# A two-block transformer forward pass on one core: tokens scaled and split without GpSimd, six units ahead, attention scores of two heads issued alternately, norm spreads placed later, and the last K tiles done by token tile

## The chip, the cores and the metric

The kernel runs on 1 core of one Trainium2 chip. The metric is the device time of one execution in microseconds (us), the median of several runs. TensorE does matmuls, VectorE (DVE), ScalarE (ACT) and GpSimd (POOL) the elementwise work; SyncE (SP) and, after the change, ScalarE too, issue DMA transfers between HBM and the on-chip memory (SBUF). Matmuls write to PSUM, eight banks of 128 x 512 fp32.

## The reference, cut to what matters

256 tokens of width 2048 go through two blocks. The first has a mixer (an 8-head gated linear scan and a 16-head chunked attention, merged by two sigmoid gates) and a feed-forward layer `square(relu(u @ w_up)) @ w_down` of width 8192. The second has a spatial-gating branch, a 16-head neighbourhood attention, two gates again, and a feed-forward layer of width 5504 with a 3-tap convolution and a SiLU gate. Each block begins with an RMS norm of the tokens, and each feed-forward layer too; a last norm ends the block:

```python
def rms_norm(x, w):
    xf = x.astype(jnp.float32)
    y = xf * lax.rsqrt(jnp.mean(xf * xf, axis=-1, keepdims=True) + EPS)
    return (y * w.astype(jnp.float32)).astype(x.dtype)
...
h = h + mixer_block(rms_norm(h, norm_mix_w[l]), ...)
u = rms_norm(h, norm_mlp_w[l])
h = h + jnp.square(jax.nn.relu(u @ w_up[l])) @ w_down[l]
```

Everything is fp32. An attention score is `q . k / 8 + bias`, one product of 64 features per head.

## The kernel before, in words

**Precision.** A product of two fp32 matrices is made of three fp32r products. Each weight tile `raw` that a DMA brings is split into a high part `wh` (ACT, line 104) and the rest `wl` (DVE, line 105); activations are split the same way, and `mm3` (lines 122 to 131) or `group` (lines 161 to 184) multiply high by high, high by low and low by high.

**Order of the work.** `Builder.prog` is a list of `Half`s and of functions. A `Half` is one weight tile of 128 x 1024 (512 KB) and the matmuls on it: half of a *unit* (128 output features for all 256 tokens, eight K tiles, `unit_b`) or two K tiles of a *group* (512 output features for two token tiles, `group`). `run` (lines 264 to 306) walks the list; one Half is one *tick*. In a tick it issues the DMA of the Half six ticks ahead (four `raw` buffers), steps the background generators (the scan, the attentions), splits the weights of the Half three ticks ahead (four `wh`/`wl` buffers), emits the Half's matmuls, and then `flush`es what became due: evictions out of PSUM, each `delay` ticks after its unit ended, and generators that were begun earlier. All engines run through their own instructions in this order and wait for each other by semaphores.

**PSUM.** Pool `mm` has four banks for units and groups, pool `sm` four for all small products (scores, transposes, norm spreads).

**The start.** `begin` (lines 400 to 482) loads the tokens, feature-major, in pieces of two and four K tiles. `split` (lines 419 to 428) scales each K tile by the norm weight: GpSimd writes the scaled tokens `xg` (line 423), ACT or DVE write their high part `xs` (lines 427, 425), and DVE subtracts (line 428). GpSimd also adds the squares for the norm (lines 457, 474). The norm factor itself is applied later, at eviction. The first eight units (`hf`) run with `wave=4`: the first halves of four units, then their second halves.

**Norm spreads.** The per-token factor is made in columns (`rsqrt_cols`) and must be spread over a row for feature-major evictions: `cols_to_row` (lines 386 to 397) makes `diag` (DVE, line 392), multiplies it by ones (TensorE, line 393, `row`) and copies the result to `R`. It is called by `new_r` (before each feed-forward layer) and by `chain` in `second`, each three ticks after the layer began and in steps of one tick; in `chain` two scalings of the whole `h` (line 990) stand ahead of it.

**Attention.** `attention` (lines 711 to 778) makes one head per step, a step every 1.4 ticks. The scores of head `i` are two matmuls of 64 features (line 737), on partitions 0 to 63 for even heads and 64 to 127 for odd ones, into one `sm` bank. Then follow the transposes of head `i-2` (line 744), and in even steps the outputs of two heads (line 751), issued alternately into the two halves of the output partitions.

**The end.** The second feed-forward layer goes in chunks of `FF2_CHUNKS` hidden tiles: `up(c+1)` stands ahead of `down(c)`. `down` of the last chunk evicts with `finish` (squares, multiplication by the norm weight), and `last` makes the norm, scales and stores.

## Time and profile before

| what | value |
| --- | --- |
| median of 3 runs | 2847.3 us (2846.12 to 2847.81) |
| the profiled execution | 2845.72 us |
| its span, first to last instruction | 2843.6 us |
| mean granted TensorE clock | 0.995 |
| busy share: TensorE, DVE, ACT, GpSimd | 98 %, 63 %, 49 %, 5 % |
| DMA | 529.52 MB, mean 186 GB/s |

The span is the time from the first to the last instruction of the core; the execution's own time is 2.1 us longer. "PE" is TensorE's matmuls, "PEld" its weight loads, which overlap them. A row of the timeline gives the start, the length, the engine, the line, the operation, its output and inputs, the count of like instructions merged, and in brackets the idle time before it with what ended that. Lengths of matmuls are from issue to the last result, so two neighbours overlap; their distance from start to start is what they cost.

### The profile page before, as it was taken

Reading aid. Unit: us, or ns where it says so; the run is one execution under the profiler, and the core shown is the slowest. Engines: PE = TensorE matmul, PEld = TensorE weight load, DVE = VectorE, ACT = ScalarE, POOL = GpSimd, SP = SyncE. Lnnn points to the kernel's source line nnn. Section 1 sums busy time; section 2 is a strip of 40 time slices with the busy share of each in tenths; the row PEclk is TensorE's granted clock in tenths of the full one; section 3 lists DMA queues with packets and bytes.
Section 4 is the critical chain, followed back from the end, with each engine's and each line's share of the span. In section 5 each row is a group of like instructions: output and inputs, shape, how many; then the busy total and the mean of one; then the engine's idle time right before and its main releaser. Section 6 shows DMA issues by size and latency. Waiting matters only on the chain.

```text
span 2843.6 us, 37303 instructions
## 1 busy us (share of the span) xinstructions
PE 2800.7 (98%) x14148; PEld 2352.9 (83%) x14148; DVE 1795.4 (63%) x2440; ACT 1390.7 (49%) x1922; POOL 129.2 (5%) x91
## 2 busy tenths in 40 slices
PE   7999999999999999999999999999999999999998
PEld 6889877888888888888887887788888888888886
DVE  6767565555576666666665755555558767676765
ACT  4554545444544444444464445544456545454544
POOL 5021000000000000000020000000000000000001
PEclk9999999999999999999999999999999999999999
DMA  6544565666556666666556665566656565556664
GB/s 199 189 156 142 165 192 160 187 192 219 181 183 190 191 192 187 192 190 189 192 192 200 205 195 187 155 192 192 216 174 188 186 192 186 191 187 188 190 188 160
DMA packets 147924, 529.52 MB, mean 186 GB/s; under 512 B 16544, under 2 KB 18848, under 8 KB 147232
## 3 DMA queue, kind: packets, MB, share of 16 engines
q1 hardware_dynamic: 147744, 527.14, 58.9%
q8 instruction: 111, 1.82, 0.3%
q14 instruction: 69, 0.57, 0.1%
HBM read 522.88 MB, written 4.19 MB: 185 GB/s over the span
## 4 chain that ended last, share of the span: by engine, by line
PE 97%; ACT 1%; DVE 0%; issue 0%; DMA 0%; POOL 0%; SPq 0%; ACTq 0%; DVEq 0%; POOLq 0%
PE mm L130 26%; PE mma L177 17%; PE mma L179 17%; PE mma L178 17%; PE mm L131 13%; PE mm L128 2%; PE s L737 1%; PE sc L638 1%; PE mm L127 1%; PE pt L744 1%; PE tr L196 1%; PE po L751 1%; DMA raw<-in_w_in_hf 0%; ACT wh L104 0%; DVE wl L105 0%
## 5 line engine op out<-in xcount | busy, mean ns | idle before, releaser
L105 DVE TENSOR_TENSOR wl<-raw,wh 128x1024 fp32r<-128x1024 f32 (+1 forms) x965 | 1193.6, 1239 | 963.5 <-ACT wh L104 954.1
L104 ACT ACTIVATE wh<-raw 128x1024 fp32r<-128x1024 f32 (+1 forms) x965 | 1018.1, 1057 | 1324.4 <-PE mma L178 675.2
L130 PE MATMUL mm<-u,wh 128*128 128x512 f32 x2610 | 931.0, 399 | 0.0
L131 PE MATMUL mm<-u,wl 128*128 128x256 f32 x2610 | 733.6, 281 | 0.0
L130 PEld LDWEIGHTS mm<-u,wh 128*128 128x128 f32 x2610 | 491.1, 188 | 113.1
L131 PEld LDWEIGHTS mm<-u,wl 128*128 128x128 f32 x2610 | 493.5, 189 | 8.3
L177 PE MATMUL mma<-wh,a 128*128 128x512 f32 x856 | 333.3, 389 | 0.0
L179 PE MATMUL mma<-wl,a 128*128 128x512 f32 x856 | 333.0, 389 | 0.0
L178 PE MATMUL mma<-wh,a 128*128 128x512 f32 x856 | 333.0, 389 | 0.0
L130 PE MATMUL mm<-xs,wh 128*128 128x512 f32 x600 | 220.7, 407 | 12.1 <-DVE xs L428 12.1
L178 PEld LDWEIGHTS mma<-wh,a 128*128 128x128 f32 x856 | 160.7, 188 | 33.5
L179 PEld LDWEIGHTS mma<-wl,a 128*128 128x128 f32 x856 | 160.7, 188 | 33.3
L177 PEld LDWEIGHTS mma<-wh,a 128*128 128x128 f32 x856 | 160.7, 188 | 32.8
L131 PE MATMUL mm<-xs,wl 128*128 128x256 f32 x600 | 170.4, 284 | 7.5 <-DVE wl L105 7.5
L177 PE MATMUL mma<-wh,xs 128*128 128x512 f32 x384 | 152.6, 397 | 0.0
L177 PE MATMUL mma<-wh,u 128*128 128x512 f32 x384 | 152.5, 397 | 0.0
L178 PE MATMUL mma<-wh,u 128*128 128x512 f32 x384 | 150.1, 391 | 0.0
L179 PE MATMUL mma<-wl,u 128*128 128x512 f32 x384 | 150.0, 390 | 0.0
L178 PE MATMUL mma<-wh,xs 128*128 128x512 f32 x384 | 149.7, 390 | 0.0
L179 PE MATMUL mma<-wl,xs 128*128 128x512 f32 x384 | 149.6, 390 | 0.0
L130 PEld LDWEIGHTS mm<-xs,wh 128*128 128x128 f32 x600 | 114.8, 191 | 37.9 <-DVE xs L428 13.2
L131 PEld LDWEIGHTS mm<-xs,wl 128*128 128x128 f32 x600 | 115.4, 192 | 10.5 <-DVE wl L105 8.6
(238 smaller groups left out, 3038.3 us busy)
## 6 DMA issues: line engine op xcount, KB each, us to landing
raw<-in_w_up SPq DMA_DIRECT2D x300, 512.0 KB, 3.5
raw<-in_w_down SPq DMA_DIRECT2D x212, 512.0 KB, 3.5
raw<-in_w_in_ga SPq DMA_DIRECT2D x64, 512.0 KB, 3.5
raw<-in_w_in_gb SPq DMA_DIRECT2D x64, 512.0 KB, 3.5
raw<-in_w_br SPq DMA_DIRECT2D x64, 512.0 KB, 3.5
raw<-in_w_out SPq DMA_DIRECT2D x64, 512.0 KB, 3.5
raw<-in_w_in_av SPq DMA_DIRECT2D x32, 512.0 KB, 3.6
raw<-in_w_in_hq SPq DMA_DIRECT2D x16, 512.0 KB, 3.7
```

The costliest lines, as they stand in the source:

```text
L104: nc.scalar.activation(hi, src, AF.Copy)
L105: nc.vector.tensor_tensor(lo, src, hi.bitcast(F32), ALU.subtract)
L127: nc.tensor.matmul(out[:, :T], lhsT=wl, rhs=x[:, 0, :], start=False, stop=False)
L128: nc.tensor.matmul(out, lhsT=wh, rhs=both, start=start, stop=True)
L130: nc.tensor.matmul(out, lhsT=wh, rhs=both, start=start, stop=False)
L131: nc.tensor.matmul(out[:, :T], lhsT=wl, rhs=x[:, 0, :], start=False, stop=False)
L177: nc.tensor.matmul(ps, lhsT=xt[:, 1, ts], rhs=wh[:, w], start=kt == 0, stop=False)
L178: nc.tensor.matmul(ps, lhsT=xt[:, 0, ts], rhs=wh[:, w], start=False, stop=False)
L179: nc.tensor.matmul(ps, lhsT=xt[:, 0, ts], rhs=wl[:, w], start=False, stop=kt == n_k - 1)
L196: self.nc.tensor.transpose(ps[:, j * T + tt * P : j * T + (tt + 1) * P], z[tt][:, c : c + P], self.ident)
L638: nc.tensor.matmul(ps[:, hh * P : (hh + 1) * P], lhsT=lhs, rhs=rhs, start=True, stop=True)
L737: nc.tensor.matmul(ps[:, sl[tt]], lhsT=aq[off : off + 64, j, tt * P : (tt + 1) * P], rhs=ak[off : off + 64, j, 0 : n(tt)], start=True, sto ...
```

## The change

It has five parts.

1. **Start.** ACT alone scales the tokens into `xg` (new `scaled`), DVE alone casts the high part and subtracts (`split`); GpSimd takes no part, and DVE adds the squares, later. The loads stand in another order: two weight Halves more come ahead of the last token tiles. The first wave is six units, of which two use `sm` banks, and the norm chain begins at tick 6 in place of 5.
2. **Norm spreads.** One tick later in `new_r`, two ticks later in `chain` of `second`, where the scaling of `h` now comes behind the spread, one tile per tick. The first units of a wave are evicted up to two ticks later to fit.
3. **Scores.** In even steps both heads' scores are issued, alternately, into two banks; odd steps issue none.
4. **Chunks.** `[8, 8, 8, 8, 8, 3]` becomes `[8, 8, 8, 8, 7, 2, 2]`.
5. **The last chunk** makes the four products of token tile 0 first and keeps its weights, then those of tile 1; norm, scaling and store go by token tile, and stores are issued from SP and ACT.

The diff, cut to its core:

```diff
-FF2_CHUNKS = [8, 8, 8, 8, 8, 3]
+FF2_CHUNKS = [8, 8, 8, 8, 7, 2, 2]
...
-                    box["ps"] = self.mm_p.tile([P, 512], F32, tag="mm", name=self.name("mm"))
+                    box["ps"] = self.sm("mms") if small else self.mm_p.tile([P, 512], F32, tag="mm", name=self.name("mm"))
...
+        def scaled(a, n):
+            for kt in range(a, a + n):
+                nc.scalar.activation(part(xg, kt, 1), part(x, kt, 1), AF.Copy, scale=self.cv("norm_mix_w", kt))
+
         def split(a, n):
-            tiles, j = st["x"][a // 4], a % 4
-            for kt in range(a, a + n):
-                src, g = x[kt // 8][:, kt % 8, :], self.cv("norm_mix_w", kt)
-                nc.gpsimd.tensor_scalar(xg[kt // 8][:, kt % 8, :], src, g, None, ALU.mult)
-                if kt % 2:
-                    nc.vector.tensor_scalar(tiles[:, kt % 4, 0, :], src, g, None, ALU.mult)
-                else:
-                    nc.scalar.activation(tiles[:, kt % 4, 0, :], src, AF.Copy, scale=g)
-            nc.vector.tensor_tensor(tiles[:, j : j + n, 1, :], xg[a // 8][:, a % 8 : a % 8 + n, :], tiles[:, j : j + n, 0, :].bitcast(F32), ALU.subtract)
+            hi, lo = (st["x"][a // 4][:, a % 4 : a % 4 + n, i, :] for i in range(2))
+            nc.vector.tensor_copy(hi, part(xg, a, n))
+            nc.vector.tensor_tensor(lo, part(xg, a, n), hi.bitcast(F32), ALU.subtract)
...
         load(0, 2)
+        load(2, 2)
         dma(0, 1)
-        load(2, 2)
         load(4, 4)
         dma(1)
         dma(2)
+        dma(3)
         load(8, 4)
-        dma(3)
         load(12, 4)
...
         def squares():
-            split(12, 4)
-            square(2)
-            yield
-            square(3)
-            yield
+            for q in (2, 3):
+                scaled(4 * q, 4)
+                split(4 * q, 4)
+                yield
+            for q in range(4):
+                nc.scalar.activation(part(sq, 4 * q, 4), part(x, 4 * q, 4), AF.Square)
+                if q:
+                    nc.vector.tensor_tensor(a[0], a[0], a[q], ALU.add)
+                if q % 2:
+                    yield
             for w in (512, 256):
-                nc.gpsimd.tensor_tensor(a[0][:, :w], a[0][:, :w], a[0][:, w : 2 * w], ALU.add)
+                nc.vector.tensor_tensor(a[0][:, :w], a[0][:, :w], a[0][:, w : 2 * w], ALU.add)
...
-        self.add(lambda: self.later(5, chain))
-        self.units([b("hf", "zf", h, delay=2 if h == 0 else 1) for h in range(8)], wave=4)
+        self.add(lambda: self.later(6, chain))
+        self.units([self.unit_b(w["hf"], h, x, self.ev("zf", h), max(1, 3 - h), h in (4, 5)) for h in range(8)], wave=6)
...
         for i in range(16 + 4):
+            if i < 16 and i % 2 == 0:
+                pss = [self.sm("s") for _ in range(2)]
+                for tt in range(2):
+                    for off, ps in zip((0, 64), pss):
+                        nc.tensor.matmul(ps[:, sl[tt]], lhsT=aq[off : off + 64, i // 2, tt * P : (tt + 1) * P],
+                                         rhs=ak[off : off + 64, i // 2, 0 : n(tt)], start=True, stop=True)
             if i < 16:
-                off, j = 64 * (i % 2), i // 2
-                ps = self.sm("s")
-                for tt in range(2):
-                    nc.tensor.matmul(ps[:, sl[tt]], lhsT=aq[off : off + 64, j, tt * P : (tt + 1) * P], rhs=ak[off : off + 64, j, 0 : n(tt)],
-                                     start=True, stop=True)
+                ps = pss[i % 2]
...
         self.rsqrt_cols(y, x)
         yield
+        yield
         yield from self.cols_to_row(y)
...
             self.rsqrt_cols(ra, xa)
             yield
+            yield
...
             st["rc"] = c
             yield
+            yield
+            yield from self.cols_to_row(c)
             h = st.pop("h")
             st.pop("nf")
             for tt in range(2):
+                yield
                 nc.vector.tensor_scalar(h[tt], h[tt], ra[:, tt : tt + 1], None, ALU.mult)
                 nc.sync.dma_start(self.x1[:, tt, :], h[tt])
-            yield from self.cols_to_row(c)
...
+        def ending(n, x):
+
+            def products(tt, nn):
+                ps = (self.sm("mms") if tt else self.mm_p.tile([P, 512], F32, tag="mm", name=self.name("mme")))
+                wh, wl = kept[nn]
+                for kt in range(2):
+                    w, ts = slice(kt * 512, kt * 512 + 512), slice(tt * P, (tt + 1) * P)
+                    nc.tensor.matmul(ps, lhsT=x(kt)[:, 1, ts], rhs=wh[:, w], start=kt == 0, stop=False)
+                    nc.tensor.matmul(ps, lhsT=x(kt)[:, 0, ts], rhs=wh[:, w], start=False, stop=False)
+                    nc.tensor.matmul(ps, lhsT=x(kt)[:, 0, ts], rhs=wl[:, w], start=False, stop=kt == 1)
+                self.later(0, lambda: finish(tt, nn, ps))
+
+            def go(wh, wl):
+                kept[n] = (wh, wl)
+                products(0, n)
+                if n == 3:
+                    for nn in range(4):
+                        products(1, nn)
+            return go
+
+        def finish(tt, n, ps):
...
+            nc.vector.tensor_tensor(h, ps, h, ALU.add)
+            self.sum_squares(st["ss"][:, tt, n : n + 1], h)
+            if n < 3:
+                nc.gpsimd.tensor_tensor(h, h, nf, ALU.mult)
+                return
+            x, r = self.col("ms", 1), self.col("rs", 1)
+            nc.vector.tensor_reduce(out=x, in_=st["ss"][:, tt, :], op=ALU.add, axis=AX.X)
+            nc.vector.tensor_scalar(x, x, 1.0 / D, None, ALU.mult)
+            self.rsqrt_cols(r, x, False)
+            nc.vector.scalar_tensor_tensor(out=h, in0=h, scalar=r, in1=nf, op0=ALU.mult, op1=ALU.mult)
+            z = st["h"][tt]
+            nc.scalar.activation(z[:, 0:1024], z[:, 0:1024], AF.Copy, scale=r)
+            nc.vector.tensor_scalar(z[:, 1024:1536], z[:, 1024:1536], r, None, ALU.mult)
+            nc.sync.dma_start(io["out"][:, tt, 1024:2048], z[:, 1024:2048])
+            nc.scalar.dma_start(io["out"][:, tt, 0:1024], z[:, 0:1024])
```

What the change does to the order on an engine, at three places. First ACT from the program's start, before (`x` are the tokens, `xs` their split parts, `xsq` squares):

```order
L104 ACTIVATE wh_129<-raw_111 128x512
L427 ACTIVATE xs_105<-x_101,cvec 128x256
L104 ACTIVATE wh_129<-raw_111 128x512
L427 ACTIVATE xs_105<-x_101,cvec 128x256
L427 ACTIVATE xs_106<-x_101,cvec 128x256 x2
L104 ACTIVATE wh_156<-raw_117 128x1024
L455 ACTIVATE xsq_154<-x_101 128x1024
```

and changed:

```order
L104 ACTIVATE wh_129<-raw_111 128x512
L421 ACTIVATE xg_103<-x_101,cvec 128x256 x4
L104 ACTIVATE wh_129<-raw_111 128x512
L421 ACTIVATE xg_103<-x_101,cvec 128x256 x4
L104 ACTIVATE wh_149<-raw_117 128x1024
L104 ACTIVATE wh_153<-raw_119 128x1024
L104 ACTIVATE wh_165<-raw_121 128x1024
```

ACT now scales all of the first eight K tiles where it scaled four, and three whole weight tiles follow with no square between.

Second DVE at the head of the second block, from the split of a weight tile through the second norm factor (`rb`, `rcol`) to the spread, before:

```order
L105 TENSOR_TENSOR wl_2319_12332<-raw_2295_12229,wh_2318_12331 128x1024
L382 TENSOR_REDUCE ms_2320_12347<-ss_2233_11932 128x2
...
L984 TENSOR_TENSOR rcol_2322_12351<-ra_2315_12320,rb_2321_12350 128x2
L105 TENSOR_TENSOR wl_2326_12366<-raw_2302_12255,wh_2325_12365 128x1024
L990 TENSOR_SCALAR h_1017_5491<-h_1017_5491,ra_2315_12320 128x2048
L990 TENSOR_SCALAR h_1018_5492<-h_1018_5492,ra_2315_12320 128x2048
L392 TENSOR_SCALAR diag_2327_12385<-ident_96,rcol_2322_12351 128x128 x2
```

and changed:

```order
L105 TENSOR_TENSOR wl_2319_12321<-raw_2295_12218,wh_2318_12320 128x1024
L105 TENSOR_TENSOR wl_2322_12339<-raw_2302_12244,wh_2321_12338 128x1024
L382 TENSOR_REDUCE ms_2323_12354<-ss_2233_11921 128x2
...
L986 TENSOR_TENSOR rcol_2325_12358<-ra_2315_12309,rb_2324_12357 128x2
L105 TENSOR_TENSOR wl_2329_12373<-raw_2307_12274,wh_2328_12372 128x1024
L105 TENSOR_TENSOR wl_2332_12391<-raw_2317_12318,wh_2331_12390 128x1024
L392 TENSOR_SCALAR diag_2333_12406<-ident_96,rcol_2325_12358 128x128 x2
```

Two scalings of `h` left the stretch ahead of `diag`, and two weight splits, one for each tick that the spread moved, came into it.

Third TensorE in an even step of the first attention, before (`s` scores, `pt` transposes, `po` outputs; the step ahead of it has two more `s` rows of the other head):

```order
L737 MATMUL s_609_3461<-ak_412_2501,aq_330_2004 128x128
L737 MATMUL s_609_3461<-ak_412_2501,aq_330_2004 128x256
L744 MATMUL pt_610_3464<-ident_96,sc_596_3413 128x128 x3
L751 MATMUL po_611_3468<-pts_594_3408,av_533_3095 64x256
L751 MATMUL po_611_3468<-pts_604_3447,av_533_3095 64x256
L751 MATMUL po_611_3468<-pts_594_3408,av_533_3095 64x128
L751 MATMUL po_611_3468<-pts_604_3447,av_533_3095 64x128
```

and changed:

```order
L735 MATMUL s_609_3450<-ak_412_2490,aq_330_1993 128x128
L735 MATMUL s_610_3451<-ak_412_2490,aq_330_1993 128x128
L735 MATMUL s_609_3450<-ak_412_2490,aq_330_1993 128x256
L735 MATMUL s_610_3451<-ak_412_2490,aq_330_1993 128x256
L744 MATMUL pt_611_3456<-ident_96,sc_597_3405 128x128 x3
```

The two heads' scores now stand side by side in the way that the two heads' outputs (`po`) stood before, and the odd step has only its `pt`.

## Rows read from the trace of the kernel before

**Rows 1.** The page, section 1, TensorE's row: busy time, share, instructions.
```profile
PE 2800.7 (98%) x14148; PEld 2352.9 (83%) x14148; DVE 1795.4 (63%) x2440; ACT 1390.7 (49%) x1922; POOL 129.2 (5%) x91
```

**Rows 2.** Waits of TensorE: waited for, us in total, times, longest us.
```profile
PE row L393 <- DVE diag L392: 10.5, 3, 6.8
PE mm L131 <- DVE wl L105: 7.5, 2, 6.2
```

**Rows 3.** Timeline of TensorE near the start (columns as above).
```profile
15.44 0.80 PE L130 MATMUL mm<-xs,wh 128*128 128x512 f32 x1 [3.05 <-DVE xs L428]
...
19.00 0.40 PE L130 MATMUL mm<-xs,wh 128*128 128x512 f32 x1
...
19.35 0.40 PE L130 MATMUL mm<-xs,wh 128*128 128x512 f32 x1
```

**Rows 4.** Timelines of DVE and of GpSimd (POOL) near the start.
```profile
28.54 3.37 DVE L428 TENSOR_TENSOR xs<-xg,xs 128x1024 fp32r<-128x1024 f32 x1 [1.72 <-POOL xg L423]
31.83 9.00 DVE L105 TENSOR_TENSOR wl<-raw,wh 128x1024 fp32r<-128x1024 f32 x4
41.03 1.23 DVE L105 TENSOR_TENSOR wl<-raw,wh 128x1024 fp32r<-128x1024 f32 x1 [0.19 <-ACT wh L104]
...
28.48 5.62 POOL L457 TENSOR_TENSOR xsq<-xsq,xsq 128x1024 f32<-128x1024 f32 x2
```

**Rows 5.** Timeline of ACT near the start.
```profile
9.21 0.91 ACT L427 ACTIVATE xs<-x,cvec 128x256 fp32r<-128x256 f32 x2 [1.42 <-DMA x<-in_xT]
...
19.09 1.06 ACT L104 ACTIVATE wh<-raw 128x1024 fp32r<-128x1024 f32 x1 [1.20 <-DMA raw<-in_w_in_hf]
```

**Rows 6.** Windows: stretch and length; busy us of each engine; granted clock; DMA.
```profile
35.24:39.26 4.02, 4.02 (x13) 3.44 (x14) 4.02 (x3) 0.00 (x0) 3.94 (x3) 0.50 0.59 160
...
776.80:780.00 3.20, 3.17 (x18) 2.83 (x19) 1.35 (x2) 0.00 (x0) 0.00 (x0) 1.00 0.67 183
...
1496.70:1503.60 6.90, 3.52 (x8) 2.82 (x9) 4.79 (x7) 0.14 (x1) 0.00 (x0) 0.51 0.69 272
...
2121.40:2124.80 3.40, 3.40 (x13) 2.92 (x12) 0.03 (x1) 0.00 (x0) 0.00 (x0) 0.50 0.77 266
...
2770.00:2831.00 61.00, 60.90 (x270) 50.11 (x269) 37.41 (x47) 26.93 (x39) 6.42 (x6) 1.00 0.50 160
```

**Rows 7.** Timeline at the head of the second block.
```profile
1497.07 2.48 DVE L990 TENSOR_SCALAR h<-h,ra 128x2048 f32<-128x2048 f32 x2
...
1500.08 1.19 PE L393 MATMUL row<-diag,ones 128*128 128x256 f32 x2 [6.76 <-DVE diag L392]
```

**Rows 8.** Attention: pieces of the critical chain (start, us, what), then TensorE's timeline.
```profile
386.00 0.85 PE s L737 x4
...
1722.96 1.06 PE s L737 x4
...
1744.12 1.01 PE po L751 x8
...
1744.05 0.44 PE L751 MATMUL po<-pts,av 128*64 128x256 f32 x2
...
1742.41 0.70 PE L737 MATMUL s<-ak,aq 64*128 64x256 f32 x2
```

**Rows 9.** Timeline of an odd step of the second attention.
```profile
1773.43 1.13 PE L737 MATMUL s<-ak,aq 64*128 64x256 f32 x4
...
1777.05 0.62 DVE L776 TENSOR_SCALAR sc<-sc,den 128x256 f32<-128x256 f32 x2
```

**Rows 10.** The end: DVE's timeline, then the transfers of `out` by that tensor.
```profile
2819.95 1.28 DVE L896 TENSOR_TENSOR h<-mma,h 128x512 f32<-128x512 f32 x2
...
2834.84 1.42 DVE L1158 TENSOR_SCALAR h<-h,rs 128x1024 f32<-128x1024 f32 x2
...
L1159 SPq DMA_DIRECT2D out<-h x4: 343/610/1121, 2835.6 to 2837.4; - x4
...
DMA to landing us min/median/max: 2.6/4.0/4.8
```

More of the change, by code (lines that the diff above doesn't have):

```diff
@@ L373, in rsqrt_cols @@
         nc.vector.tensor_scalar(x, x, EPS, None, ALU.add)
-        t = self.col("nw")
+        t = self.col("nw", x.shape[-1])
         nc.vector.tensor_tensor(t, y, y, ALU.mult)
@@ L446, in begin @@
         prep(0, 0)
+        scaled(0, 2)
         split(0, 2)
+        scaled(2, 2)
+        split(2, 2)
         prep(0, 1)
[L449 removed]
+        scaled(4, 4)
         split(4, 4)
[L451 to L457 removed]
         prep(1)
[L460 removed]
         prep(2)
[L462 removed]
         dma(4)
         dma(5)
[L465 removed]
+        sq = [self.big("xsq") for _ in range(2)]
+        a = [part(sq, 4 * q, 4).rearrange("p k t -> p (k t)") for q in range(4)]
         def squares():
[L468 to L475 removed]
+            for q in (2, 3):
[8 more added lines that the diff above has]
+                    yield
+            for w in (512, 256):
+                nc.vector.tensor_tensor(a[0][:, :w], a[0][:, :w], a[0][:, w : 2 * w], ALU.add)
+            st["acc"] = a[0][:, :T]
+            yield
             nc.gpsimd.tensor_copy(self.masks, m)
@@ L924, in up @@
         def up(c):
-            self.units([self.unit_b(io["w_up"], c * CHUNK + i, self.x_of("u"), ev_up(c, i)) for i in range(CHUNK)],
-                       wave=0 if c else 4)
+            self.units([self.unit_b(io["w_up"], c * CHUNK + i, self.x_of("u"), ev_up(c, i), 1 if c else max(1, 3 - i))
+                        for i in range(CHUNK)], wave=0 if c else 4)
         def finish(n, h):
@@ L1115, in finish @@
+        def finish(tt, n, ps):
+            s = slice(n * 512, (n + 1) * 512)
+            h, nf = st["h"][tt][:, s], st["nf"][:, s]
+            if n == 0 and tt == 0:
                 st["ss"] = self.new_sums()
                 nc.scalar.preload_act_table_set("natural_log_exp_and_others")
-            for tt in range(2):
-                self.sum_squares(st["ss"][:, tt, n : n + 1], h[tt])
-            for tt in range(2):
-                (nc.vector if n == 3 else nc.gpsimd).tensor_tensor(h[tt], h[tt], st["nf"][:, n * 512 : (n + 1) * 512], ALU.mult)
@@ L1129, in down @@
                 pairs = n_k // 2
-                at = 2 * starts[c] + n * pairs
+                at = 4 * sum(k // 2 for k in sizes[:c]) + n * pairs
                 srcs = [io["w_down_2"][at + i] for i in range(pairs)]
                 if n_k % 2:
-                    srcs.append(io["w_down_2_last"][n])
-                self.group(srcs, n_k, x, self.add_down(n, finish if c == n_c - 1 else None))
+                    srcs.append(io["w_down_2_odd"][n])
+                if c < n_c - 1:
+                    self.group(srcs, n_k, x, self.add_down(n))
+                else:
+                    self.add(Half(srcs[0], HALF, ending(n, x)))
             self.add(lambda: acts.pop(c - 1, None))
@@ L1146, in ffn2 @@
             down(c)
-    def last(self):
-        nc, st, io = self.nc, self.st, self.io
-        x, r = self.mean_square(st.pop("ss")), self.col("rs")
-        self.rsqrt_cols(r, x, False)
-        for i in range(4):
-            tt, s = i % 2, slice(1024 * (i // 2), 1024 * (i // 2) + 1024)
-            z = st["h"][tt][:, s]
-            if i % 2:
-                nc.scalar.activation(z, z, AF.Copy, scale=r[:, tt : tt + 1])
-            else:
-                nc.vector.tensor_scalar(z, z, r[:, tt : tt + 1], None, ALU.mult)
-            nc.sync.dma_start(io["out"][:, tt, s], z)
     def build(self):
@@ L1167, in build @@
             self.run()
-            self.last()
 def _b16(w):
@@ L1229, in _layout @@
     a["w_down_2"] = _down(w, FF2_CHUNKS)
-    a["w_down_2_last"] = np.ascontiguousarray(w[-P:].reshape(P, 4, 512).transpose(1, 0, 2))
+    odd = np.cumsum(FF2_CHUNKS)[[n % 2 for n in FF2_CHUNKS].index(1)] * P
+    a["w_down_2_odd"] = np.ascontiguousarray(w[odd - P : odd].reshape(P, 4, 512).transpose(1, 0, 2))
     lb = f("lb_logits")
```

26 lines of the change are left out of this document (7 added, 19 removed).

## The prediction

> **What bounds the kernel now.** I read the page first: TensorE is busy for 2800.7 us, 98 % of the span [rows 1]. A change can therefore pay in three ways only: fewer idle spots of TensorE, fewer stretches at half clock, less work on it. TensorE's waits come next: 10.5 us on `diag` of the norm spreads, 7.5 on low weight parts [rows 2]. The timelines of TensorE, DVE, GpSimd and ACT near the start show where the second comes from, and a wait on the split tokens ahead of it [rows 3 to 5]. The windows show what such a wait costs beyond its own length: after 6.18 us of idling up to 35.24 TensorE works for 4 us at a granted clock of 0.50, its lower level of 1.2 GHz; around the spread at 1500 it is busy 3.52 us at that level, after the spread at 2120 3.40 [rows 6]. Last I read the attention stage for the scores [rows 8, 9], and the end [rows 10].
>
> Two lengths are used throughout. A tick of a unit has eight K tiles 0.35 apart, 19.00 to 19.35 [rows 3]: 2.8 us. A tick of a group has twelve matmuls; 270 took 60.9 us [rows 6], so 2.7.
>
> **The start: 11.2 us less.** Three things fall away.
> (a) The fifth K tile of the first weight starts at 15.44, after 3.05 us of waiting for DVE's subtraction, which waited for GpSimd's scaling [rows 3, 4]. Its tokens landed by 9.21, when ACT began [rows 5]. After the change ACT makes four scalings (0.91 for two [rows 5]), done at about 11.0; DVE casts 1024 columns, somewhere between 0.71 (one-source operation of L1158, 1.42 for two [rows 10]) and 1.23 (two-source L105 [rows 4]), and subtracts for 1.23. So the tile can start at about 12.9, 2.5 earlier.
> (b) TensorE waits 7.5 us for low weight parts (L131) [rows 2]. DVE makes them, and was held by GpSimd: a subtraction took 3.37 and four weight splits 9.00, beside GpSimd's adds of 5.62, where a split alone takes 1.23 [rows 4]. With GpSimd out, the fifth weight, which landed at 19.09 [rows 5], is split by 19.1 + 1.06 + 1.23 = 21.4, while TensorE, four weights of 2.8 and the slow clock behind 12.9, comes to it after 24. I count the whole 7.5.
> (c) Without that wait the 4.02 us at half clock go [rows 6], worth 2.0.
> Against this, the first rise of the clock: it came between 15.44, where a matmul takes 0.80, and 19.00, where it takes 0.40 [rows 3]. After unbroken work from 12.9 it may come just as late in absolute time, costing up to 1.7; I take half, 0.85. The sum: 2.5 + 7.5 + 2.0 - 0.85 = 11.15. DVE's new casts and adds of squares (5 adds) lie beside six first halves of 2.8, and the wave of six gives every later weight 2 to 5 us. Bounds: 8 (the casts cost more and a later weight waits 2) and 13.
>
> **The norm spreads: 12.0 us less.** A spread moved by one tick has 2.8 more, but one more weight split (1.23) ahead of `diag` on DVE. For the two feed-forward norms, which wait 1.88 each (what 10.5 leaves beside 6.76 [rows 2, 7]): 1.88 + 1.23 - 2.8 = 0.3 each. At the second block two ticks of a group (5.4) are gained, the two scalings of `h`, 2.48 [rows 7], leave the way and two splits come into it: 6.76 + 2.46 - 2.48 - 5.4 = 1.3. So about 2.0 of 10.5 stays: 8.5 less. The half-clock stretches behind the waits of 6.76 and of 2120 go with them, 3.52/2 + 3.40/2 = 3.5 [rows 6]; after the wait at 777 the granted clock stays at 1.00 [rows 6], so I expect no loss after shorter ones. 8.5 + 3.5 = 12.0. The units evicted later hold their `mm` banks longer: the bank for the fifth unit comes free in the tick in which it is wanted, which I cost at nothing because the three evictions stand ahead of DVE's weight splits for a tick that is still three ahead. If that cover is gone, TensorE waits one eviction, below 1.3, three times. Bounds: 8 and 14.
>
> **The scores: 15.3 us less.** A head's scores cost 0.85 in the first attention and 1.06 in the second, x4 in the rows because an fp32 matmul goes in two passes [rows 8]. Sixteen heads each: 16 x 0.85 + 16 x 1.06 = 30.6. TensorE is the bound in these stages, so what a pair saves is saved in the time. Two heads use different halves of the array's rows and write to two banks. The nearest row is `po`, whose two heads use different halves of the columns and are issued alternately: two passes end after 0.44, eight after 1.01, so each further pair of passes costs (1.01 - 0.44)/3 = 0.19 [rows 8]; in `s` two passes take 0.70 and four 1.13, 0.215 for one [rows 8, 9]. There, two passes of different heads cost one slot. If rows do as columns do, a pair costs what one head did: 8 x 0.85 + 8 x 1.06 = 15.3, half is saved. If they don't overlap, only the edge of one group is saved: 1.06 is four passes of 0.215 and 0.2 beside; eight passes and one edge are 1.92 in place of 2.12, in the first attention 1.50 in place of 1.70: 16 x 0.2 = 3.3. I take 15.3, the row that is nearest; bounds 3.3 and 16.
> A rule of the Trainium skill ("TensorE: Matmul & The Clock Gate", Part 3, "The mechanism") speaks against half of this order: matmuls start and end strictly in program order, and only different row groups overlap; the passes of one matmul are on one row group, so the second would hold up the next matmul. The row of `po` doesn't show that, having eight passes in four slots.
>
> **The end: 0.4 us less.** With chunks of 2 the products of `down` come as soon as four `up` halves are done, and their `mm` bank was emptied only one tick before. I estimate ACT's `wh` 1.06 [rows 5], DVE's `wl` 1.23 [rows 4], about 1.0 of SiLU operations and an add of 0.64 (1.28 for two [rows 10]) ahead of it on DVE: 3.9 against a tick of 2.7, so 1.2 where it happens in full, 1.9 in all over three places. Bounds: 0 and 5. Behind the last matmul only one token tile is left: one add (0.64) and one scaling (0.71 of L1158) less on the way, and stores on two queues, where four issues ran from 2835.6 to 2837.4 on one [rows 10]: one issue gap of 0.6 and some 0.3 of the landing (2.6 to 4.8). Together 2.3. 2.3 - 1.9 = 0.4; bounds 3 slower, 4 faster. The same weights pass through TensorE in all chunks, so their sizes alone cost nothing.
>
> **Sum.** 11.2 + 12.0 + 15.3 + 0.4 = 38.9. The profiled execution took 2845.7, so 2806.8; it lies 1.6 below the median, so 2808.4, given as 2808.
>
> **The rivals.**
> *Scores don't overlap*: no row shows two groups of 64 array rows at work at once, since `s` was always issued one head at a time; `po` alternates columns, not rows. 12 less gained: 2820. Chance 0.12.
> *Strict order of passes*: A, then A's second beside B's first, and so on: five slots of eight. 5 x 0.215 + 0.2 = 1.28 and, with two short slots, 1.06: 8 x 0.84 + 8 x 0.64 = 11.9 in place of 15.3: 2811. Chance 0.06; the eight passes of `po` in 1.01 speak against it. The rule named above gives this time.
> *The start stays bound*, now by ACT, which makes all 16 scalings and every high part, or by the loads' new order: it gains 6 in place of 11: 2813. Chance 0.06. Against it: ACT idles 1.42 before the scalings and 1.20 before the weight [rows 5].
> *The short chunks let the clock fall*: waits at two of them bring 3.4 us at half clock each, 3.4 us lost: 2811. Chance 0.04.
> *Slower*: an odd step of an attention now begins with `pt`, no scores ahead of it, and a head's `pt` stands one step behind its probabilities. From an odd step's start to the next `pt` there will be the step's own `pt` (about 0.5, half of a head's scores as I estimate), a tick of 2.8 and the pair's scores, 1.06: 4.4. The probabilities were done 4.24 after a step's start, 1773.43 to 1777.67 [rows 9]. Only 0.2 is spare. If DVE or ACT come later than before, a pair may lose 1.9 in waiting, as a spread does, and 1.7 by half clock behind it: 16 pairs lose 58: 2865. It decides from 45/16 = 2.8 a pair. Against it: the scores of an odd head lie ready a whole step early, which takes `s` out of that 4.24, and steps with two ticks between them have 2.8 more. Chance 0.02.
>
> **How the numbers follow.** The forecast has 0.70, with 2803 to 2813 as its own range. A change below 0.2 % (5.7 us) can't be told from none here. The range ends at 2821 with the scores that don't overlap, and at 2800 where all four parts reach their upper bounds: 2847.3 - 13 - 14 - 16 - 4 = 2800; start, spreads and end at their lower bounds together (8, 8, -3) give 2819, inside it. Faster: every case but the last, and what an unforeseen wait takes: 0.96; the same 0.02; slower 0.02.
>
> **What would show it.** TensorE's wait on `diag` is about 2 us in place of 10.5; from about 12.9 it works without a gap, and no half clock appears near 35, 1500 and 2121. The eight passes of a pair of scores take 1.06 in the second attention. Waits on L897's add appear at the short chunks, under 2 us. The last stores go out on two queues. I am wrong if the passes take 1.9, if TensorE's waits move to other tiles in the attentions, or if the wait for `wl` near 35 stays.

## The result and the profile after

The changed kernel takes 2806.3 us (median of 4 runs, 2805.9 to 2807.2), against 2847.3 (2846.1 to 2847.8) before: a ratio of 0.9857, 95% interval 0.9840 to 0.9874, 41.0 us less. The forecast was 2808 in a range from 2800 to 2821. The profiled execution's span went from 2843.6 to 2804.7 us, which is 38.9 less: the profiled execution of the kernel before lay 1.6 below its median, that of the changed kernel 0.3 above.

First the page's busy line of the changed kernel, then its table of TensorE's waits (waited for, us in total, times, longest):

```profile
PE 2779.1 (99%) x14148; PEld 2341.2 (83%) x14148; DVE 1793.8 (64%) x2456; ACT 1392.8 (50%) x1932; POOL 96.6 (3%) x70
```

```profile
PE mm L130 <- DVE xs L426: 6.9, 1, 6.9
PE mm L130 <- ACT wh L104: 3.1, 1, 3.1
PE pt L744 <- DVE sc L776: 1.8, 2, 0.9
PE row L393 <- DVE diag L392: 1.6, 3, 1.2
PE mma L177 <- DVE h L897: 1.0, 1, 1.0
PE mme L1127 <- DVE h L897: 0.5, 1, 0.5
```

TensorE's busy time fell by 21.6 us [rows 1]: scores that run beside each other, and less time at half clock. The wait for `diag` is 1.6 in place of 10.5, the one for `wl` is gone [rows 2]. Four small waits are new, at `pt`, `mma` and `mme`, 3.3 together.

Where the time went can be read off from one kind of instruction that both kernels issue equally often and in the same tick: ACT's weight split, L104, 965 times. The n-th in one trace set against the n-th in the other gives, at quiet places, how far the changed kernel is ahead:

| stretch, ended by | before, us | ahead, us | gained in it | forecast |
| --- | --- | --- | --- | --- |
| start, split 120 | 389.66 | 11.89 | 11.9 | 11.2 |
| first attention, split 200 | 639.34 | 18.93 | 7.0 | 6.8 |
| norm of the first feed-forward layer, split 260 | 811.48 | 20.48 | 1.6 | 1.6 |
| head of the second block, split 520 | 1543.69 | 27.66 | 7.2 | 7.2 |
| second attention, split 640 | 1916.44 | 35.85 | 8.2 | 8.5 |
| norm of the second feed-forward layer, split 760 | 2257.86 | 38.88 | 3.0 | 3.3 |
| end, to the last matmul | 2830.90 | 36.82 | -2.1 | -1.9 |
| behind the last matmul, to the span's end | 2843.6 | 38.9 | 2.1 | 2.3 |

(The forecast's 15.3 and 12.0 are split here by its own working: 8 x 0.85 and 8 x 1.06; 1.6, 5.4 + 1.8, and 1.6 + 1.7.)

**The start.** Timelines of TensorE and of DVE in the changed kernel:

```profile
13.36 0.76 PE L130 MATMUL mm<-xs,wh 128*128 128x512 f32 x1 [3.11 <-ACT wh L104]
...
17.34 0.63 PE L130 MATMUL mm<-xs,wh 128*128 128x512 f32 x1
17.98 0.44 PE L130 MATMUL mm<-xs,wh 128*128 128x512 f32 x1
18.38 0.40 PE L130 MATMUL mm<-xs,wh 128*128 128x512 f32 x1
```

```profile
11.26 0.69 DVE L425 CAST xs<-xg 128x1024 fp32r<-128x1024 f32 x1 [2.11 <-ACT xg L421]
11.99 1.23 DVE L426 TENSOR_TENSOR xs<-xg,xs 128x1024 fp32r<-128x1024 f32 x1
13.13 3.49 DVE L105 TENSOR_TENSOR wl<-raw,wh 128x1024 fp32r<-128x1024 f32 x3
```

The fifth K tile starts at 13.36 (15.44 before [rows 3]). The table of waits names ACT's `wh`, which had been ready for long; it was the subtraction that ended at 13.22. The cast cost 0.69, the low end of the two prices. Three weight splits then take 3.49, 1.16 each, where four took 9.00 [rows 4], and TensorE has no further gap before 454.

**The scores.** TensorE's timeline in the second attention, an even step, an odd one and the next even one:

```profile
1712.27 1.14 PE L735 MATMUL s<-ak,aq 64*128 64x256 f32 x8
1713.33 0.66 PE L744 MATMUL pt<-ident,sc 128*128 128x128 f32 x4
1713.92 1.08 PE L751 MATMUL po<-pts,av 128*64 128x256 f32 x8
1720.55 0.60 PE L744 MATMUL pt<-ident,sc 128*128 128x128 f32 x4
1723.85 1.13 PE L735 MATMUL s<-ak,aq 64*128 64x256 f32 x8
```

Eight passes take 1.14, as long as four took [rows 9]. From the even step's `s` to its `pt` it is 1.06, the price of one head [rows 8].

### The profile page after: what moved, and what is told of

Same layout as the page of the kernel before. It is cut to its first block, busy times and chain, and to the rows that moved or that the text cites. A ratio compares the mean times of both kernels' runs of the same rounds, so it can differ in the third digit from the quotient of the medians.

```text
span 2804.7 us, 37286 instructions
## 1 busy us (share of the span) xinstructions
PE 2779.1 (99%) x14148; PEld 2341.2 (83%) x14148; DVE 1793.8 (64%) x2456; ACT 1392.8 (50%) x1932; POOL 96.6 (3%) x70
## 3 DMA queue, kind: packets, MB, share of 16 engines
q10 hardware_dynamic: 288, 1.05, 0.1%
## 4 chain that ended last, share of the span: by engine, by line
PE 98%; ACT 1%; DVE 0%; DMA 0%; issue 0%; SPq 0%; DVEq 0%; ACTq 0%
PE mm L130 26%; PE mma L177 17%; PE mma L178 17%; PE mma L179 17%; PE mm L131 13%; PE mm L128 2%; PE sc L636 1%; PE mm L127 1%; PE tr L196 1%; PE s L735 1%; PE pt L744 1%; PE po L751 1%; ACT wh L104 0%; PE mms L130 0%; DMA x<-in_xT 0%
## 5 line engine op out<-in xcount | busy, mean ns | idle before, releaser
L104 ACT ACTIVATE wh<-raw 128x1024 fp32r<-128x1024 f32 (+1 forms) x965 | 1017.9, 1057 | 1286.5 <-PE mma L178 661.1
L177 PE MATMUL mma<-wh,a 128*128 128x512 f32 x840 | 327.2, 390 | 1.0 <-DVE h L897 1.0
L178 PE MATMUL mma<-wh,a 128*128 128x512 f32 x840 | 326.8, 389 | 0.0
L179 PE MATMUL mma<-wl,a 128*128 128x512 f32 x840 | 326.8, 389 | 0.0
L130 PE MATMUL mm<-xs,wh 128*128 128x512 f32 x570 | 208.7, 405 | 10.1 <-DVE xs L426 6.9
L177 PEld LDWEIGHTS mma<-wh,a 128*128 128x128 f32 x840 | 157.7, 188 | 33.7 <-DVE h L897 1.4
L178 PEld LDWEIGHTS mma<-wh,a 128*128 128x128 f32 x840 | 157.7, 188 | 32.5
L131 PE MATMUL mm<-xs,wl 128*128 128x256 f32 x570 | 161.1, 283 | 0.0
L130 PEld LDWEIGHTS mm<-xs,wh 128*128 128x128 f32 x570 | 108.7, 191 | 34.3 <-issue 6.9
L131 PEld LDWEIGHTS mm<-xs,wl 128*128 128x128 f32 x570 | 109.2, 192 | 1.8
```

The source lines that it names most:

```text
L104: nc.scalar.activation(hi, src, AF.Copy)
L130: nc.tensor.matmul(out, lhsT=wh, rhs=both, start=start, stop=False)
L131: nc.tensor.matmul(out[:, :T], lhsT=wl, rhs=x[:, 0, :], start=False, stop=False)
L177: nc.tensor.matmul(ps, lhsT=xt[:, 1, ts], rhs=wh[:, w], start=kt == 0, stop=False)
L178: nc.tensor.matmul(ps, lhsT=xt[:, 0, ts], rhs=wh[:, w], start=False, stop=False)
L179: nc.tensor.matmul(ps, lhsT=xt[:, 0, ts], rhs=wl[:, w], start=False, stop=kt == n_k - 1)
```

## The experiments

Each run's kernel is the changed one with one edit, or with several where that is said. The kernel before, timed beside them, had medians of 2847.6, 2846.9 and 2845.9 in the three sets, and 2847.3 beside the changed kernel, so medians of different sets that lie under about 2 us apart aren't told apart by the times alone; for those the traces are read. "By the weight splits" means the same count as in the table above, against the trace of the changed kernel.

### The scores: overlap, and what it needs

```diff
-            if i < 16 and i % 2 == 0:
...
+            if i < 16:
+                off, j = 64 * (i % 2), i // 2
+                ps = self.sm("s")
+                for tt in range(2):
+                    nc.tensor.matmul(ps[:, sl[tt]], lhsT=aq[off : off + 64, j, ...
```

> The changed kernel, but each head's scores issued alone in its own step, as before the change. Theory (two heads on different halves of the array's rows work at once when issued alternately, and TensorE is the bound there): the gain of the two attentions comes back, 7.05 + 8.19 as the two traces stand apart, so 15.2 slower than the changed kernel, 2821.5; the two waits of pt on sc (0.8 and 0.95) vanish, since the odd step's scores again stand ahead of pt. Rival (no overlap, only fewer groups with an edge of 0.2 each): 3.3 slower, 2809.6. Rival (the gain came from other places that shifted): under 2 slower.

2822.6 us (2821.0 to 2822.9), 16.3 slower, and no wait on `pt`. By the weight splits the two stages lose 7.0 and 8.2, what they had gained; most of the rest, 0.9, lies at the start, whose program is the same in both (see the last section). Overlap holds; fewer edges alone would have made 3.3.

```diff
-                for tt in range(2):
-                    for off, ps in zip((0, 64), pss):
+                for off, ps in zip((0, 64), pss):
+                    for tt in range(2):
```

> The changed kernel with both heads' scores in the even step and in two banks, but all matmuls of the first head ahead of all of the second. Theory (overlap needs the alternate order, since matmuls start in program order and the passes of one head share their rows): at most the last pass of the first head runs beside the first of the second, a pair costs 1.70 in place of 1.06 and 1.28 in place of 0.86, 8 x 0.64 + 8 x 0.42 = 8.5 slower, 2814.8; with no overlap at all 12 slower, 2818.3. Rival (the engine looks far enough ahead to overlap in any order): 2806.3. Rival (the gain lies in the regrouping alone): 2806.3 as well, and a pair still takes 1.06 and 0.86; the length of the eight passes tells the two apart from no overlap.

2806.5 us (2806.2 to 2806.8): no difference from the changed kernel. Its timeline, one even step:

```profile
1712.36 1.14 PE L735 MATMUL s<-ak,aq 64*128 64x256 f32 x8
1713.43 0.66 PE L744 MATMUL pt<-ident,sc 128*128 128x128 f32 x4
```

My theory fell. All four passes of the first head stand ahead of the second head's four in the program, and still the eight take 1.14: in the trace they start two by two, at 1712.355 and 1712.368, 1712.675 and 1712.688, and so on, 13 ns apart (7 ns with the alternate order). The rows don't name the head of a pass; but issued alone, in the kernel before, the passes of one head start 0.215 or more apart in this attention, so the two of a pair are of different heads. So the second head's first pass started beside the first head's first, ahead of three passes that stand before it in the program. What the change needed was both heads next to each other, not alternately. The rule quoted in the prediction from the Trainium skill ("TensorE: Matmul & The Clock Gate", Part 3, "The mechanism"), matmuls starting strictly in program order, doesn't hold in this run; the measurement decides. (What the prediction gives as the other half of the rule, that only different row groups overlap, the Trainium skill says there of weight loads beside matmuls in flight, not of matmuls.)

### The start: what held TensorE back

```diff
-                    nc.vector.tensor_tensor(a[0], a[0], a[q], ALU.add)
+                    nc.gpsimd.tensor_tensor(a[0], a[0], a[q], ALU.add)
...
-                nc.vector.tensor_tensor(a[0][:, :w], a[0][:, :w], a[0][:, w : 2 * w], ALU.add)
+                nc.gpsimd.tensor_tensor(a[0][:, :w], a[0][:, :w], a[0][:, w : 2 * w], ALU.add)
```

> The changed kernel with the five adds of squares at the start on GpSimd, as before, and all else as changed. Theory (GpSimd's adds slow DVE's two-source operations, so weight splits at the start come late): DVE's splits beside the adds take 2 to 3 us each in place of 1.23, TensorE waits for wl again between 24 and 40, 4 to 10 slower with a stretch at half clock, 2810 to 2816. Rival (DVE was late because it waited for GpSimd's scaled tokens in its own order; the adds hurt nothing, since the weights have 2 to 5 us to spare): the splits beside the adds are longer but TensorE doesn't wait, at most 0.5 slower.

2812.5 us (2811.7 to 2812.7), 6.2 slower. From the table of waits, and the timelines of DVE and GpSimd:

```profile
PE rs L330 <- POOL xsq L471: 4.2, 1, 4.2
```

```profile
28.58 10.35 DVE L105 TENSOR_TENSOR wl<-raw,wh 128x1024 fp32r<-128x1024 f32 x4 [0.20 <-ACT wh L104]
...
27.38 6.62 POOL L467 TENSOR_TENSOR xsq<-xsq,xsq 128x1024 f32<-128x1024 f32 x2
```

The size is what the theory gave, the place is not. Beside the adds a split takes 2.59 on average in place of 1.23 (10.35 / 4), and GpSimd's adds 3.3 each, but no matmul waits for `wl`. What waits is `rs`, the norm's product, for GpSimd's sum: 4.18, and a stretch at half clock behind it, up to 41.0. The slowing of DVE agrees with the Trainium skill ("SBUF — State Buffer", "SBUF: two separate sides"): one of VectorE's operations with two inputs in SBUF and a GpSimd operation that reads it exclude each other. In the trace they take turns: GpSimd's add of 30.73 ends at 33.99, and the split that started at 31.66 ends at 35.08, 1.09 behind it, about the length of a split alone.

```diff
         def split(a, n):
-            hi, lo = (...
-            nc.vector.tensor_copy(hi, part(xg, a, n))
+            for kt in range(a, a + n):
+                nc.gpsimd.tensor_scalar(xg[kt // 8][:, kt % 8, :], src, g, None, ALU.mult)
...
```

> The changed kernel with only the scaling and split of the tokens as before (GpSimd makes xg, ACT and DVE scale for the high parts), the squares still added by DVE, the loads and the wave of six as changed. Theory (the chain through GpSimd and the sharing of DVE with it both cost): the fifth K tile starts 2 us later, at 15.4, and DVE's subtractions of the last tokens wait for GpSimd with weight splits queued behind them, so TensorE waits for wl again, 2 to 8 with a stretch at half clock: 4 to 11 slower, 2810 to 2817. Rival (only the first tiles are held; the wave of six and the loads' order give the rest its room): 1.5 to 2.5 slower, 2808 to 2809, and no wait for wl.

2809.1 us (2809.0 to 2809.5), 2.8 slower, 3.3 by the weight splits, and no wait for `wl`: the rival, just above its 2808 to 2809. The fifth tile starts at 15.36, 2.0 later, and, which the rival didn't have, `rs` waits 1.3 for the sum of squares, whose adds come late behind the subtractions.

The two edits together:

> The changed kernel with both the scaling of the tokens and the adds of squares on GpSimd, as before, but the loads, the wave of six and the chain's tick as changed. Theory (each costs by itself, one at the first tiles, one at the norm chain that waits for the sum): 2.8 and 6.2 as the two single runs have it, 9.0 slower, 2815.3, and TensorE waits on rs, not on wl. Rival (together they hold DVE so that weight splits come late, as in the kernel before): waits for wl return and it is 11 to 14 slower, 2817 to 2820. Rival (the waits overlap, since GpSimd's adds start when its scalings are done): 6 slower, 2812.

2812.9 us (2812.1 to 2813.8), 6.7 slower, 7.4 by the weight splits. Its table of waits, DVE's and GpSimd's timelines, and the window behind the wait (stretch, length, then the busy times of each engine, granted clock, DMA):

```profile
PE mms L131 <- DVE wl L105: 3.4, 1, 3.4
```

```profile
26.20 3.41 DVE L431 TENSOR_TENSOR xs<-xg,xs 128x1024 fp32r<-128x1024 f32 x1 [1.72 <-POOL xg L426]
29.54 6.68 DVE L105 TENSOR_TENSOR wl<-raw,wh 128x1024 fp32r<-128x1024 f32 x2
...
26.14 2.39 POOL L472 TENSOR_TENSOR xsq<-xsq 128x1024 f32<-128x1024 f32 x1
28.61 6.52 POOL L472 TENSOR_TENSOR xsq<-xsq,xsq 128x1024 f32<-128x1024 f32 x2
```

```profile
32.90:36.00 3.10, 3.04 (x10) 2.66 (x11) 3.10 (x1) 0.00 (x0) 3.02 (x2) 0.50 0.49 170
```

Here the picture of the kernel before [rows 4, 6] is back: DVE's last subtraction waits 1.72 for GpSimd's tokens and then runs into GpSimd's adds (3.41), the weight splits stand behind it and are slowed too, TensorE waits for `wl` and works on at half clock, up to 38.6. With the loads and the wave of six as changed, a wait for `wl` takes both jobs. The wait is 3.4 where it was 6.2. No expectation met both parts: the waits are those of the first rival, the time (6.7) is nearest to the last. The prices don't add up (2.8 and 6.2 singly) because `rs` no longer waits at all: held up by `wl` and the half clock, TensorE comes to it only at 41.0, when GpSimd's sum is done since 39.0. And with both jobs back, some 4.5 of the 11.9 us won at the start stay won. No run undoes the order of the loads, or the wave of six beside GpSimd's jobs, so how these share the 4.5 isn't shown.

```diff
-        self.add(lambda: self.later(6, chain))
-        self.units([self.unit_b(w["hf"], h, x, self.ev("zf", h), max(1, 3 - h), h in (4, 5)) for h in range(8)], wave=6)
+        self.add(lambda: self.later(5, chain))
+        self.units([self.unit_b(w["hf"], h, x, self.ev("zf", h), 2 if h == 0 else 1) for h in range(8)], wave=4)
```

> The changed kernel with the first wave of four units, no unit in the small banks, the norm chain at tick 5 and the first eviction after two ticks, as before; ACT and DVE split the tokens as changed. Theory (without GpSimd the splits are early enough; the wave of six was room that is hardly needed): TensorE comes to the second halves at 25.3, when the eighth to eleventh tile are split since 18.5, the last since 23.9 and the fifth weight since 21.4; only the sum of squares, done at 31.9, is late for a chain at tick 5, which comes at 31.0: 0.5 to 2 slower, 2806.8 to 2808.3, with a wait on rs. Rival (the room of the two ticks is what took the waits for wl away): waits for wl near 26 and 35 again, 5 or more slower, above 2811.

2808.0 us (2807.9 to 2808.0), 1.7 slower, no wait for `wl`, and 1.56 on `rs`: the theory. Without GpSimd the six units give room to the norm chain, not to the weights.

### The norm spreads

```diff
         self.rsqrt_cols(y, x)
         yield
-        yield
         yield from self.cols_to_row(y)
...
             self.rsqrt_cols(ra, xa)
             yield
-            yield
...
             st["rc"] = c
             yield
-            yield
-            yield from self.cols_to_row(c)
             h = st.pop("h")
             st.pop("nf")
             for tt in range(2):
-                yield
                 nc.vector.tensor_scalar(h[tt], h[tt], ra[:, tt : tt + 1], None, ALU.mult)
                 nc.sync.dma_start(self.x1[:, tt, :], h[tt])
+            yield from self.cols_to_row(c)
```

and the first units of both feed-forward layers evicted after one tick again.

> The changed kernel with all norm spreads as before (one and two ticks earlier, both scalings of h ahead of the spread, evictions of the first units after one tick). Theory (the spread is late by DVE's queue, and a wait of 1.9 or more may bring a stretch at half clock): 1.55 + 7.18 + 3.03 = 11.8 slower, 2818.1, with TensorE's waits for diag at 10.5 in three places. Rival (the stretches at half clock were chance and don't come back): 8.9 slower, 2815.2. Rival (the later evictions cost something that this gives back): under 7 slower.

2817.9 us (2817.8 to 2818.6), 11.6 slower, with 10.5 of waits for `diag` in the same lengths. The windows behind the first and the third spread:

```profile
758.00:761.50 3.50, 3.50 (x14) 2.96 (x13) 1.01 (x2) 0.00 (x0) 0.00 (x0) 0.59 0.78 214
2094.40:2098.00 3.60, 3.60 (x21) 3.12 (x20) 1.05 (x2) 0.39 (x1) 0.00 (x0) 1.00 0.68 205
```

In this run the clock fell after the first wait of 1.88 and not after the third; in the trace of the kernel before it was the other way round [rows 6]. By the weight splits the three places lose 3.0, 7.1 and 1.6, where the change had gained 1.6, 7.2 and 3.0. The sum agrees, the two smaller terms have changed places.

```diff
             yield
             yield
-            yield from self.cols_to_row(c)
             h = st.pop("h")
             st.pop("nf")
             for tt in range(2):
-                yield
                 nc.vector.tensor_scalar(h[tt], h[tt], ra[:, tt : tt + 1], None, ALU.mult)
                 nc.sync.dma_start(self.x1[:, tt, :], h[tt])
+            yield from self.cols_to_row(c)
```

> The changed kernel with both scalings of h ahead of the spread again at the head of the second block, with the later ticks kept. Theory (DVE's queue sets diag): the wait for diag there is 1.22 + 2.48 = 3.7 in place of 1.22, 2.5 slower, and 4.2 if a stretch at half clock of 3.4 us follows; 2808.8 to 2810.5. Rival (DVE has idle time ahead of diag in that tick that takes the scalings in): 0 slower, 2806.3.

2811.2 us (2810.0 to 2811.4), 4.9 slower, above the 2810.5 of the theory. The wait is 3.59 in place of 1.22, 2.4 more, as DVE's queue has it; the half clock behind it lasts longer than I had allowed, from the wait's end at 1481.5 to about 1487.5, worth 2.8 by the weight splits (5.2 in all).

### The end

The end as before (chunks of 8, 8, 8, 8, 8, 3, one norm, four stores from one queue):

```diff
-FF2_CHUNKS = [8, 8, 8, 8, 7, 2, 2]
+FF2_CHUNKS = [8, 8, 8, 8, 8, 3]
...
-                    self.add(Half(srcs[0], HALF, ending(n, x)))
+                self.group(srcs, n_k, x, self.add_down(n, finish if c == n_c - 1 else None))
```

> The changed kernel with the end as before: chunks 8, 8, 8, 8, 8, 3, the last products for both token tiles together, one norm, four stores from one queue. Theory (the short chunks lose as much in waits for banks as the shorter tail gains: 2.07 lost up to the last matmul, 2.1 won behind it): the same within 0.5 us, 2805.8 to 2806.8, TensorE's waits on the add of L897 gone and the tail behind the last matmul 12.7 in place of 10.6. Rival (the end gains on its own, and the 2.07 belongs to something else): 2 slower, 2808.3.

2806.3 us (2806.1 to 2807.1): no difference, as expected. Its last matmul ends at 2791.5 and 12.9 follow; in the changed kernel 2794.1 and 10.7. 0.5 of the 2.6 us was there before the end, from the start; 2.1 is the end's own.

```diff
-ps = (self.sm("mms") if tt else self.mm_p.tile([P, 512], F32, tag="mm", name=self.name("mme")))
+ps = (self.mm_p.tile([P, 512], F32, tag="mm", name=self.name("mme")) if tt else self.sm("mms"))
...
-                    self.group(srcs, n_k, x, self.add_down(n))
+                    self.group(srcs, n_k, x, self.add_down(n), 0 if n_k == 2 else 1)
```

> The changed kernel, with the evictions of two-tile chunks in the tick in which their products end, and with the last chunk's first products in the pool of small banks (which lies idle then) and its second in the other. Theory (the two waits of 0.98 and 0.49 are for banks whose eviction comes a tick late): both vanish, 1.5 to 2.0 faster, 2804.3 to 2804.8. Rival (DVE's queue is the limit there, 9 tenths busy in these ticks, so the add that stands earlier makes the next weight split late instead): the wait moves to wl, within 0.5 us of the changed kernel.

2805.2 us (2804.5 to 2805.3), 1.1 below both the changed kernel and the run with the end as before. From its table of waits:

```profile
PE mms L1127 <- DVE a L105: 0.3, 1, 0.3
```

Both waits for banks are gone, a new one of 0.3 has come. Against the weight splits in mid-layer it gains 1.5 up to the last matmul: the waits were for banks, not for DVE's queue.

### Towards a faster version

```diff
-        scaled(4, 4)
-        split(4, 4)
+        for at in (4, 6):
+            scaled(at, 2)
+            split(at, 2)
```

> The changed kernel with tokens' tiles 4 to 7 scaled and split in two pairs in place of one four. Theory (the chain ACT, cast, subtract behind the load sets the fifth tile): it starts at 9.53 + 0.91 + 0.43 + 0.69, about 11.7 in place of 13.36, 1.6 faster, 2804.7; if the clock rises no earlier than now, 18.0, half of that, 2805.5. Rival (the weight splits behind the subtraction on DVE become the bound, since two pairs take 0.3 more): under 0.3 faster.

2805.7 us (2805.3 to 2806.4); the runs overlap with those of the changed kernel, so no gain is shown. In its trace the tokens came only at 10.34 (9.53 in the changed kernel), the tile started at 12.58, 0.8 earlier, and the clock rose only at about 18.4, not at 18.0; by the weight splits 0.15 of the 0.8 is left. What the pairs are worth stays open within these shifts.

The three edits together, with this one at the tail:

```diff
                 self.later(0, lambda: finish(tt, nn, ps))
+                if (tt, nn) in ((1, 0), (1, 3)):
+                    self.later(0, lambda: norm(nn // 3))
```

> The changed kernel with the pairs of tiles at the start, the banks at the end as in end_banks, and at the end the first token tile's norm put behind one add of the second tile in place of ahead of all. Theory (the three are independent): 1.6 for the pairs, 1.1 for the banks as measured, and 0.8 for the tail, where four squares stood in a row from 2791.4 to 2793.8 and GpSimd's multiplication stretched an operation of one column to 1.04: 3.5 faster, 2802.8. Rival (the norm of the first tile is only pushed into the second's): 2.7 faster, 2803.6.

2804.4 us (2803.5 to 2805.0), 1.8 below the changed kernel, with no run of the one in the range of the other, but in different sets. The fifth tile starts at 11.69 here and the clock rises at about 16.1; by the weight splits the start is 1.6 ahead, which is also as much as starts of one program differ (last section). The end's banks give 1.5 again, as in the run before; that part holds. The tail gives nothing: 11.0 from the last matmul to the end, 10.7 in the changed kernel. The first tile's norm was only pushed into the second's, the rival. Timeline of DVE at the tail of the changed kernel and of this one:

```profile
2792.75 2.48 DVE L1146 TENSOR_TENSOR h<-mms,h 128x512 f32<-128x512 f32 x4
...
2797.00 1.05 DVE L375 TENSOR_TENSOR nw<-rs 128x1 f32<-128x1 f32 x1
```

```profile
2791.47 1.88 DVE L1149 TENSOR_TENSOR h<-mme,h 128x512 f32<-128x512 f32 x3
...
2795.11 0.38 DVE L375 TENSOR_TENSOR nw<-rs 128x1 f32<-128x1 f32 x1
```

Three adds still stand in a row behind the first tile's norm, which itself was now slowed (an operation on one column took 0.99 in place of 0.16 beside GpSimd).

## Why the prediction was right

- **Bound.** That only TensorE's waits, clock and work count held everywhere: the terms add up, to 38.9 forecast and 38.9 in the two traces. That they meet so closely is luck: errors inside the terms cancel, as told below, and the start alone differs by up to 1.6 between executions of one program. The 1.7 between 2808 and 2806.3 is mostly the 1.6 by which the forecast raised its sum to the median.
- **Start, 11.2 forecast, 11.9 measured.** (a) 2.1 in place of 2.5: the tile could start at 13.36 and not 12.9, mostly since its tokens landed at 9.53 and not 9.21. (b), (c) By matched matmuls the two waits for `wl` and their clock were worth 9.9, not 9.5. The clock rose at 17.98, and only 0.4 of the 2.1 was lost by that, where 0.85 had been set against it. The reason in (b) was half right: with the wave of six in place, GpSimd's share of DVE alone didn't make the weights late, nor did its scaling alone; both together did, and cost 7.4 of the 11.9. Each alone cost time too: the adds 6.2, at the norm's product `rs`, and the scaling 2.8, at the fifth tile and at `rs`. A wait on `rs` was in none of the prediction's terms.
- **Spreads, 12.0 forecast, 11.8 measured.** The sum of DVE's queue gave the waits to within 0.2: 0.2, 1.2 and 0.2 in place of 0.3, 1.3 and 0.3. The half clock counted was the one seen in that execution; as spread_before shows, which of the two waits of 1.88 brings it changes from trace to trace, so that it came behind one of them was in the sum only because the trace had it.
- **Scores, 15.3 forecast, 15.2 measured, with two errors that cancel.** The new waits at `pt`, 0.81 and 0.95, weren't in the sum; they are the rival on the slower side in small, once in each attention and not in each pair, and the prediction's own sign of being wrong, waits that move to other tiles in the attentions, in a size that didn't matter. Without them a pair saves 0.98 and 1.14, 0.1 more than one head's price. And the reason was incomplete: `po` pointed to the right time, but the alternate order isn't what makes it. (In the case without overlap, 16 x 0.2 is 3.2, not 3.3.)
- **End, 0.4 forecast, 0.0 measured.** 2.1 lost and 2.1 won, against 1.9 and 2.3. Of the 2.1 lost, 1.47 are the two waits for banks; the rest isn't placed. The 2.1 won has its size by luck. ACT's scaling in the trace before, and in the changed one with the last store that it issues (ACTq):

```profile
2834.82 2.19 ACT L1156 ACTIVATE h<-h,rs 128x1024 f32<-128x1024 f32 x2 [0.68 <-DVE rs L377]
```

```profile
2798.53 1.15 ACT L1157 ACTIVATE h<-h,rs 128x1024 f32<-128x1024 f32 x1 [1.56 <-DVE rs L377]
2799.71 0.35 ACTq L1160 DMA_DIRECT2D out<-h  x1
```

From the last matmul to this scaling it took 3.92 before (from 2830.90) and 4.45 in the changed kernel (from 2794.08): 0.5 longer, where the forecast had one add of 0.64 less. The adds of the second tile stand behind the first tile's norm, and a GpSimd multiplication slowed one step of the norm by 0.9. From the scaling to the last issue, at 2837.4 before [rows 10] and here at 2799.71, 2.6 became 1.2, about as forecast (0.71 and 0.6); from there to the end 6.2 became 5.0, where 0.3 had been set for the landing.

- **Rivals.** None of those with a chance of their own came about; scores_alone rules out the first, scores_in_turn the second.

## What to carry to other kernels

Where one engine is busy 98 %, cost a change place by place by counting what stands ahead of the awaited instruction on its engine; an order that is moved by a tick is worth the tick less the work that comes in between. Two small products on different row halves, into two banks, belong next to each other on TensorE; of the two orders tried, both served. Two jobs of a helper engine that meet one queue don't cost the sum of their single prices (6.2 and 2.8 alone, 6.7 together here), and the wait can appear at another place, so undo such jobs singly and together. A term that comes out can still be made of wrong parts: split the measured term as the forecast was split.

## What the runs showed of the hardware that I had not expected

- Matmuls of two heads on different halves of the array's rows overlap even with three other passes between them in the program: 8 passes in 1.14, starts 13 ns apart in place of 7.
- After waits of the same length, 1.88, the granted clock fell to 0.50 in one place and stayed at 1.00 in another, and the two places changed roles between the traces of two kernels.
- A DVE operation on one column took 1.05 in place of 0.16 beside a GpSimd multiplication, at 2797.00.
- The first rise of the clock has no fixed distance from the first unbroken work. With the same start of the program the fifth tile began at 13.36 and 13.42, and the clock rose at about 18.0 in the changed kernel, at about 16.4 in end_before. That makes 0.7 us between executions of one program start. Over the seven traces with the same start (the changed kernel, the two runs on scores, the two on spreads, end_before and end_banks) the clock rose between 16.4 and 19.0, and at the 60th weight split they lie 1.6 apart, from 0.7 ahead of the changed kernel to 0.9 behind it: more than a small edit there is worth.
